# Two-layer FoX and MLA trunk on one core: piecewise first loads, division by head, another bank, another order of end projections, dummy transposes

## The chip, the cores and the metric

The kernel runs on one NeuronCore of a Trainium2 chip, in one launch. The metric is the device time of an execution in microseconds (us); lower is better. All matrix products are made of float32 operands that are each split into two fp32r parts.

## What is computed

A trunk of two layers over x of shape (1, 256, 1024). Each layer is four post-normed steps, with `ALPHA` = sqrt(2):

```python
for i in range(DEPTH):                       # DEPTH = 2, FoX in layer 0, MLA in layer 1
    if i == N_A:
        k_nope, k_rope, v_shared = shared_kv(x, kv_w_down, kv_norm, kv_w_up, cos, sin)
    x = post_norm(x, 0.5 * swiglu(x, ffn1_w_in[i], ffn1_w_out[i]), ...)      # d_ff = 2816
    x = post_norm(x, fox_mixer(...) if i < N_A else mla_mixer(...), ...)     # 16 heads each
    x = post_norm(x, 0.5 * swiglu(x, ffn2_w_in[i], ffn2_w_out[i]), ...)
    gate = sigmoid(x @ ple_w_gate[i] + ple_b_gate[i])
    x = post_norm(x, gate * (p[i] @ ple_w_proj[i]), ...)
```

`swiglu` is `(silu(x Wg) * (x Wu)) Wo`. `fox_mixer` is causal softmax attention with a decay from cumulated log-sigmoids added to the logits; `mla_mixer` takes its keys and values from a shared compressed latent.

## The kernel before, in words

**Numbers.** A float32 operand v is kept as `hi` (v rounded to fp32r, a copy on ScalarE) and `lo` (v minus hi, a subtraction on VectorE). A product is three matmuls, hi·hi, hi·lo and lo·hi, summed in PSUM (`mm3`, L412; all matmuls are recorded at L420, in `mm`). So each weight is loaded, copied on ACT (L140) and subtracted on DVE (L141) before PE can use both parts.

**The weight stream.** `Stream` loads the weights in the order in which a dry run (`Recorder`) saw them used. A group of 1 MB goes from HBM into one of three raw buffers (tile `raw`) by DMAs on SyncE's queue; for FFN input weights (`win`) that is one DMA for the gate columns and one for the up columns. Only the first two groups are loaded in finer pieces: two row blocks (k) per DMA, four DMAs of 256 KB each. A group holds two units; a unit is two row blocks of 128 rows by 512 columns. `split` (L123) turns a unit into the parts in one of up to 14 slots (tiles `hl`, `ota`, `otb`, `qk`, `fs`), whole: one ACT instruction of 128x1024 and one DVE instruction. `use` splits what is needed at once, `pump` splits ahead when its estimates of the engines' time say that there is room; so the order of the instructions on ACT and DVE is set by that planner while the program is written out, and each engine then runs its queue in that order.

**Stages.** Tokens are two tiles t of 128. `XT(t)` transposes x of a tile on PE (eight 128x128 transposes into two `tr` banks, L424) and splits the result into `xT` (L429 on ACT, L430 on DVE). In `ffn` (L509) the first two chunks of 256 hidden columns are made by `H(c, t)` with the tokens as the stationary side (128x512 matmuls, eight row blocks times three per tile), the other nine by `HT` with the weights as the stationary side (128x256 matmuls, 96 a chunk), in the groups 2 to 4, 5 to 7 and 8 to 10; after each group come output projections `W` (128x512 matmuls). `HT` of the chunks 5 and 8 begins with `EDGE[layer, ffn]` dummy transposes of the identity into its first bank. At the program's start `setup` asks for all of x tile 0, then weight group 0, then x tile 1, then group 1, and the first `ffn` (`cold`) does H(0, 0) with `XT(1)` in its middle, then H(0, 1).

**FoX** (L719). `V(n, t)` makes values in a bank of ring `h` (two banks), and its parts on ACT and DVE free that bank. `gen_k` and `gen_q` make a head pair's keys and queries in the same ring `h`. For head pairs j = 0 to 7: `QK(j)` (scores in two `y` banks), `softmax(j)` (L855), `T(j-1)` (transposes of the probabilities, L897 for the first four), `AV(j-1)`. `softmax` takes row maxima of both heads on DVE, four exponentials with sums on ACT (L877: two segments of head 0, then two of head 1), one reciprocal of the four sums on DVE (L882), and four multiplications on GpSimd (POOL, L886).

**MLA** (L1050). For 16 heads, `softmax`, `T(h)`, `AV(h)` and `O(h, ts)`, the head's share of the output projection for the tiles ts, into y. The parts of the last two heads' AV results lie in tile `fs`. After the loop the rest is written out by hand (see the difference below): projections, T(15), AV(15), the layer norm of tile 0 (`ln`), `XT(0)`, the remaining projections of tile 1.

Of the kernel before, what the change touches and what calls it, by code (L numbers as in the profile page):

```python
# [10 lines left out]
F32 = mybir.dt.float32  # L11
# [18 lines left out]
STAG = 3  # L30
LATE = 6
HAT = 12
VAT = 12
SW_COLD = 0
SW_H00 = 0
SW_H10 = 1
SW_H01 = 2
# [9 lines left out]
    (((0, 0),), ((1, 0),), ((0, 1),)),  # L47
)
GROUPS = ((2, 3, 4), (5, 6, 7), (8, 9, 10))
EDGE = {(0, "ffn1"): 4, (0, "ffn2"): 1, (1, "ffn1"): 2, (1, "ffn2"): 1}  # L50
VT = {0: (2, (0,)), 5: (2, (1,)), 8: (3, (0,)), 10: (3, (1,))}


# [13 lines left out]
class Recorder:  # L67
# [7 lines left out]
    def pump(self, *a, **k):  # L75
        pass

    lend = reclaim = check = load = busy = pair = pump


class Stream:


    def __init__(self, nc, raw_pool, pool, loads, seq):
        self.nc, self.raw_pool, self.pool, self.loads = nc, raw_pool, pool, loads
        seen = []
        self.groups = []
        for key in seq:
            g = group_of(key)
            if g not in seen:  # L90
# [12 lines left out]
        self.raw, self.hl = {}, {}  # L103
        self.slots = [f"hl{i}" for i in range(NSLOT)]
        self.slot_of = {}
        self.kept = set()
        self.loaded = self.ready = 0
        self.done = 0
        self.pending = None
        self.pe_t = self.act_t = self.dve_t = self.dma_t = 0.0  # L110
        self.arrives = {}

    def load(self, n=NRAW):
        while self.loaded < len(self.groups) and self.loaded < self.done + n:
            g = self.groups[self.loaded]
            r = self.raw_pool.tile([128, 2048], F32, name="raw")
            self.loads(self.nc.sync, g, r, self.loaded < 2)
# [5 lines left out]
    def split(self):  # L123
# [16 lines left out]
        nc.scalar.activation(hi, src, AF.Copy)  # L140
        nc.vector.tensor_tensor(lo, src, hi.bitcast(F32), op=ALU.subtract)  # L141
# [45 lines left out]

    def pump(self):

        if self.ready == len(self.order) or not self.slots:  # L190
# [33 lines left out]
def unit_of(key, raw):  # L224

    k, u = key[0], key[-1] % 2
    if k in ("win", "fv"):
        return raw.rearrange("p (k c) -> p k c", c=512)[:, 2 * u : 2 * u + 2, :], 128, 1024
    if k in ("wout", "fo", "pg", "pp", "mo", "qr"):
        return raw[:, 1024 * u : 1024 * u + 1024], 128, 1024  # L230
    if k in ("fk", "fq"):
        return raw.rearrange("p (k c) -> p k c", c=256)[:, :, 128 * u : 128 * u + 128], 128, 1024
    if k == "ff":
        return raw[:, 0:1024], 128, 1024
    if k == "pb":
        return raw[0:1, 0:1024], 1, 1024
# [12 lines left out]

def make_loads(a):  # L250
    def rows(ap, k0, n):
        return ap[k0 * 128 : (k0 + n) * 128, :].rearrange("(k p) c -> p k c", p=128)

    def loads(q, g, raw, fine):
        k, i = g[0], g[-1]
        if k == "win":
            w = a[g[2]][0][g[1]]
            c = g[3]
            r = raw.rearrange("p (k c) -> p k c", c=512)
            n = 2 if fine else 4  # L260
            for k0 in range(0, 4, n):
                for s in range(2):
                    c0 = DFF * s + 256 * c
                    q.dma_start(
                        r[:, k0 : k0 + n, 256 * s : 256 * s + 256], rows(w[:, c0 : c0 + 256], 4 * i + k0, n)
                    )
# [69 lines left out]
class Trunk:  # L336
# [33 lines left out]
    def setup(self):  # L370
# [6 lines left out]
        self.ones = one([1, 128], F32R, "ones")  # L377
        self.xT = one([128, 2, 2, 8, 128], F32R, "xT")
        self.rope = one([128, 2, 2, 64], F32, "rope")
        self.load_x(0)  # L380
        self.S.load(1)
        self.load_x(1)
        nc.gpsimd.memset(self.mask, 0.0)
        self.spin(2)
        warm = self.tl([128, 1], F32, "ss", 2)
        nc.gpsimd.memset(self.mhalf, -0.5)
# [17 lines left out]
    def load_x(self, t):  # L404
        for h in range(2):
            self.dma(
                self.x[t][:, 512 * h : 512 * h + 512],
                None if self.rec else self.a["x"][0, 128 * t : 128 * t + 128, 512 * h : 512 * h + 512],
            )


    def mm3(self, out, lhsT, rhs, start, stop):  # L412
# [17 lines left out]
        self.nc.vector.tensor_tensor(lo, src, hi.bitcast(F32), op=ALU.subtract)  # L430
        self.S.pair(cols(src))

    def transposed(self, t, src):

        for h in range(2):
# [10 lines left out]
    def XT(self, t):  # L446
        self.transposed(t, self.x[t])

    def moving(self, ps, t, name, width, at=None, what=None, sweeps=0):

# [58 lines left out]
    def ffn(self, li, which, lni, kv=False, at=None, cold=False):  # L509
# [7 lines left out]
        def H(c, t, at=None, what=None, sweeps=0):  # L517
            ps = self.bank("h")
            self.moving(ps, t, ("win", li, which, c), 512, at, what, sweeps)
            if c not in g:  # L520
# [59 lines left out]
        if kv:  # L580
            self.kv_down(0)
        if cold:
            H(0, 0, 18, lambda: self.XT(1), SW_COLD)
            H(0, 1, sweeps=SW_H01)
            H(1, 0)
        else:
            H(0, 0, sweeps=SW_H00)
# [131 lines left out]
    def fox(self, li):  # L719
# [2 lines left out]
        S.reclaim("ota", "otb")  # L722

        def V(n, t, at=None, what=None):
            ps = self.bank("h")
            self.moving(ps, t, ("fv", n), 512, at, what, {(0, 0): SW_V00, (1, 0): SW_V10, (0, 1): SW_V01}.get((n, t), 0))
            o = self.tl([128, 2, 512], F32R, "g4", 5)
            self.parts(o[:, 0, :], o[:, 1, :], ps)
# [126 lines left out]
        def softmax(j):  # L855
# [26 lines left out]
            nc.vector.reciprocal(su, su)  # L882
            for s in range(2):
                for q, (c0, c1) in enumerate(seg):
                    i = 2 * s + q
                    nc.gpsimd.tensor_scalar(  # L886
                        P[s][:, c0:c1], P[s][:, c0:c1], su[:, i : i + 1], 1.0, op0=ALU.mult, op1=ALU.mult
                    )
            st[j] = P

        def T(j):
# [158 lines left out]
    def mla(self, li):  # L1050
# [206 lines left out]
                AV(h - 1)  # L1257
        self.load_gb(li, 1)
        O(LATE + 2, (1,))
        O(14, (0,))  # L1260
        T(15)
        AV(15)
        O(LATE + 3, (1,))
        O(15, (0,))
        self.ln(0, y[0], ALPHA, LN_EPS)
        for h in range(LATE + 4, 16):
# [5 lines left out]

    def run(self):
        S = self.S
        self.XT(0)
        self.spin(2)
# [74 lines left out]
```

## Time and profile before

| | us |
|---|---|
| Three runs | 1117.63, 1117.82, 1119.79 (median 1117.82) |
| The profiled execution | 1116.59 |
| its span, first to last instruction | 1114.8 |
| PE busy in the span | 1087.3 (98%) |
| DVE, ACT, POOL busy | 712.2, 541.6, 81.8 |
| mean granted TensorE clock | 0.993 |

A timeline row reads: start, length in us, engine, line, operation, out<-in, shape and count; in brackets the idle time of the engine ahead of it and what ended that. Rows that follow each other on one engine at one line are merged. PE's matmuls overlap in the records, so the pace of a stretch is the distance between two starts over the number of matmuls. A row of windows gives for each engine the busy time (and count), then the granted TensorE clock, the DMA share and the GB/s.

### The profile page before, as it was taken

How to read it: one execution, taken by the hardware profiler on the slowest of the kernel's cores; microseconds unless marked ns; L12 is line 12 of the kernel's file. 1: busy time of each engine (PE TensorE's matmuls, PEld its weight loads, DVE VectorE, ACT ScalarE, POOL GpSimd, SP SyncE). 2: the span in 40 equal slices, each digit the busy share in tenths (PEclk: the TensorE clock that was granted, in tenths of full speed). 3: DMA queues.
4: the chain of work that ended last, by engine and by line, in shares of the span. 5: the costliest groups of instructions: out<-in, count | busy, mean ns of one | idle time of the engine just before them, and what ended most of it. 6: DMA issues, size and time to landing. Idle time of an engine off the chain costs nothing. (4 is left out here: it accounts for less than half of the span.)

```text
span 1114.8 us, 17666 instructions
## 1 busy us (share of the span) xinstructions
PE 1087.3 (98%) x7182; PEld 982.3 (88%) x7182; DVE 712.2 (64%) x994; ACT 541.6 (49%) x786; POOL 81.8 (7%) x130
## 2 busy tenths in 40 slices
PE   8999999989999999999999999998999899999997
PEld 6999998889879989897899899987899689898986
DVE  5765545777787555457976454397766786454576
ACT  5554433566646435443565343345655455344421
POOL 0000000322200000000320000011111000000000
PEclk9999999989999999999999999999999999999999
DMA  9796652554338666454486655344443478555402
GB/s 299 240 308 212 216 188 68 171 168 152 114 113 301 200 209 199 159 175 157 155 287 229 204 186 166 88 111 145 156 123 114 158 257 278 185 190 189 164 26 76
DMA packets 150548, 199.00 MB, mean 179 GB/s; under 512 B 11714, under 2 KB 128450, under 8 KB 150468
## 3 DMA queue, kind: packets, MB, share of 16 engines
q1 hardware_dynamic: 150468, 197.88, 53.8%
q8 instruction: 56, 0.92, 0.3%
q14 instruction: 24, 0.20, 0.1%
HBM read 196.81 MB, written 1.05 MB: 177 GB/s over the span
## 5 line engine op out<-in xcount | busy, mean ns | idle before, releaser
L141 DVE TENSOR_TENSOR hl<-raw,hl 128x1024 fp32r<-128x1024 f32 (+3 forms) x295 | 349.3, 1202 | 184.8 <-ACT hl L140 183.7
L140 ACT ACTIVATE hl<-raw 128x1024 fp32r<-128x1024 f32 (+3 forms) x295 | 298.5, 1032 | 208.0 <-PE y L420 85.3
L420 PE MATMUL h<-xT,hl 128*128 128x256 f32 x2016 | 243.3, 281 | 2.4 <-DVE g L430 1.8
L420 PEld LDWEIGHTS h<-xT,hl 128*128 128x128 f32 x2016 | 237.4, 190 | 4.7 <-DVE g L430 2.0
L420 PE MATMUL y<-hl,g 128*128 128x512 f32 x816 | 189.6, 390 | 0.0
L420 PEld LDWEIGHTS y<-hl,g 128*128 128x128 f32 x816 | 152.2, 188 | 31.0
L420 PE MATMUL h<-hl,xT 128*128 128x512 f32 (+1 forms) x432 | 102.1, 387 | 3.3 <-DVE hl L141 1.9
L420 PE MATMUL tr<-xT,hl 128*128 128x256 f32 x864 | 102.5, 278 | 0.0
L420 PEld LDWEIGHTS tr<-xT,hl 128*128 128x128 f32 x864 | 100.5, 188 | 0.1
L420 PEld LDWEIGHTS h<-hl,xT 128*128 128x128 f32 x432 | 79.3, 188 | 21.2 <-DVE hl L141 3.0
L492 POOL TENSOR_TENSOR rs<-ve,mhalf 128x1 f32<-128x1 f32 x16 | 15.2, 950 | 829.4 <-DVE ve L491 829.4
L420 PE MATMUL y<-hl,xT 128*128 128x512 f32 (+2 forms) x276 | 52.6, 346 | 0.0
L420 PEld LDWEIGHTS y<-hl,xT 128*128 128x128 f32 x276 | 44.0, 188 | 6.4 <-issue 0.7
L429 ACT ACTIVATE xT<-tr 128x512 fp32r<-128x512 f32 x36 | 20.0, 596 | 57.0 <-PE tr L424 57.0
L430 DVE TENSOR_TENSOR g<-P,g 128x512 fp32r<-128x512 f32 x36 | 24.9, 693 | 34.5 <-ACT g L429 34.5
L429 ACT ACTIVATE g<-P 128x512 fp32r<-128x512 f32 x36 | 22.8, 632 | 40.1 <-DVE P L559 29.1
L420 PE MATMUL y<-hl,ota 128*128 128x512 f32 x144 | 36.1, 394 | 0.0
L141 DVE TENSOR_TENSOR otb<-raw,otb 128x1024 fp32r<-128x1024 f32 (+1 forms) x20 | 24.1, 1203 | 18.8 <-ACT otb L140 18.8
L141 DVE TENSOR_TENSOR qk<-raw,qk 128x1024 fp32r<-128x1024 f32 x21 | 25.9, 1233 | 14.3 <-ACT qk L140 14.3
L420 PE MATMUL tr<-xT,qk 128*128 128x256 f32 x264 | 31.9, 277 | 0.0
L420 PEld LDWEIGHTS tr<-xT,qk 128*128 128x128 f32 x264 | 30.9, 188 | 0.0
L430 DVE TENSOR_TENSOR xT<-tr,xT 128x512 fp32r<-128x512 f32 x36 | 23.1, 683 | 11.7 <-ACT xT L429 11.7
(222 smaller groups left out, 1349.2 us busy)
## 6 DMA issues: line engine op xcount, KB each, us to landing
raw<-in_ffn_w_in_dram SPq DMA_DIRECT2D x172, 512.0 KB, 4.9
raw<-in_ffn_w_out_dram SPq DMA_DIRECT2D x44, 1024.0 KB, 5.1
raw<-in_fox_w_in_dram SPq DMA_DIRECT2D x12, 1024.0 KB, 5.2
raw<-in_ple_w_gate_dram SPq DMA_DIRECT2D x8, 1024.0 KB, 5.0
raw<-in_mla_w_o_dram SPq DMA_DIRECT2D x8, 1024.0 KB, 5.5
gb<-in_ln_g_dram SPq DMA_DIRECT2D x8, 512.0 KB, 5.1
gb<-in_ln_b_dram SPq DMA_DIRECT2D x8, 512.0 KB, 7.7
raw<-in_fox_w_o_dram SPq DMA_DIRECT2D x4, 1024.0 KB, 4.8
```

The source lines that it names most:

```text
L140: nc.scalar.activation(hi, src, AF.Copy)
L141: nc.vector.tensor_tensor(lo, src, hi.bitcast(F32), op=ALU.subtract)
L420: self.nc.tensor.matmul(out, lhsT, rhs, start=start, stop=stop)
L429: self.nc.scalar.activation(hi, src, AF.Copy)
L430: self.nc.vector.tensor_tensor(lo, src, hi.bitcast(F32), op=ALU.subtract)
L492: nc.gpsimd.tensor_tensor(rs, ve, self.mhalf, op=ALU.pow)
```

## The change

Five edits. (1) The first two weight groups come in pieces of one row block (128 KB a DMA, eight DMAs a group instead of four), the halves of x are put between them, and the first four units are split in two halves (`FINE`); the first chunk for both tiles is written out in `first`, which takes row blocks as they come and puts the four half-`XT`s between them, with the planner on `hold`. (2) In FoX, `softmax` takes the reciprocal and the multiplications head by head. (3) `V(n, 1)` uses a bank of ring `y`. (4) In MLA's end T(15), O(9, tile 1) and AV(15) come ahead of O(14, tile 0). (5) `EDGE` of layer 1's first FFN goes from 2 to 4.

```diff
-EDGE = {(0, "ffn1"): 4, (0, "ffn2"): 1, (1, "ffn1"): 2, (1, "ffn2"): 1}
+EDGE = {(0, "ffn1"): 4, (0, "ffn2"): 1, (1, "ffn1"): 4, (1, "ffn2"): 1}
...
+        def part(c):
+            nc.scalar.activation(hi[:, c], src[:, c], AF.Copy)
+            nc.vector.tensor_tensor(lo[:, c], src[:, c], hi[:, c].bitcast(F32), op=ALU.subtract)
+
+        if self.ready < FINE:
+            part(slice(0, 1))
+            between()
+            part(slice(1, 2))
+        else:
+            part(slice(None))
...
-            n = 2 if fine else 4
+            n = 1 if fine else 4
             for k0 in range(0, 4, n):
+                if fine and (i, k0) in between:
+                    between[i, k0]()
...
-        self.load_x(0)
-        self.S.load(1)
-        self.load_x(1)
+        self.load_x(0, 0)
+        self.S.between = {
+            (0, 2): lambda: self.load_x(1, 0),
+            (1, 0): lambda: self.load_x(0, 1),
+            (1, 1): lambda: self.load_x(1, 1),
+        }
+        self.S.load(2)
...
+        def first():
+
+            ps = [self.bank("h") for _ in range(2)]
+
+            def part(t, *ks):
+                for k in ks:
+                    w = self.use(("win", li, which, 0, k // 2))
+                    for i, j in SWEEPS[0][0]:
+                        self.mm(
...
+            S.hold = True
+            self.XT(0, (0,))
+            self.spin(2)
+            S.split()
+            part(0, 0, 1)
+            S.split(lambda: self.XT(1, (0,)))
+            part(0, 2)
+            part(1, 0, 1)
+            S.split(lambda: self.XT(0, (1,)))
+            part(1, 2)
+            part(0, 3)
+            part(1, 3)
+            self.XT(1, (1,))
+            S.split()
+            part(0, 4, 5, 6, 7)
+            act(0, 0, ps[0])
+            part(1, 4, 5)
+            S.split()
+            S.split()
+            S.hold = False
+            part(1, 6, 7)
+            act(0, 1, ps[1])
...
         if cold:
-            H(0, 0, 18, lambda: self.XT(1), SW_COLD)
-            H(0, 1, sweeps=SW_H01)
+            first()
             H(1, 0)
...
-            ps = self.bank("h")
+            ps = self.bank("h" if t == 0 else "y")
...
-            nc.vector.reciprocal(su, su)
-            for s in range(2):
+
+            def divide(s):
+                nc.vector.reciprocal(su[:, 2 * s : 2 * s + 2], su[:, 2 * s : 2 * s + 2])
...
         O(LATE + 2, (1,))
+        T(15)
+        O(LATE + 3, (1,))
+        AV(15)
         O(14, (0,))
-        T(15)
-        AV(15)
-        O(LATE + 3, (1,))
         O(15, (0,))
```

What stands in the engines' queues, first PE's at the start of the program, before the change. Here x_66 and x_67 are the two tiles of x, and the four `hl` of the first rows are the four units of the first chunk.

```order
L420 MATMUL h<-hl_131,xT 128x512 x6
L420 MATMUL h<-hl_134,xT 128x512 x6
L420 MATMUL h<-hl_149,xT 128x512 x6
L424 MATMUL tr<-ident,x_67 128x128 x8
L420 MATMUL h<-hl_158,xT 128x512 x6
```

The same place of the changed kernel; its four units are hl_130, hl_144, hl_168 and hl_196.

```order
L436 MATMUL h<-hl_130,xT 128x512 x6
L440 MATMUL tr<-ident,x_67 128x128 x4
L436 MATMUL h<-hl_144,xT 128x512 x3
L436 MATMUL h<-hl_130,xT 128x512 x6
L440 MATMUL tr<-ident,x_66 128x128 x4
L436 MATMUL h<-hl_144,xT 128x512 x9
L440 MATMUL tr<-ident,x_67 128x128 x4
L436 MATMUL h<-hl_168,xT 128x512 x6
L436 MATMUL h<-hl_196,xT 128x512 x6
L436 MATMUL h<-hl_168,xT 128x512 x6
L436 MATMUL h<-hl_196,xT 128x512 x6
```

Before, all 24 matmuls of tile 0 stood ahead of those of tile 1; now 24 matmuls of both tiles on the first two units, with the second half of x between them, stand ahead of those on the third and fourth.

DVE at the first softmax of FoX, before; `tt` are the biases of the exponentials and `su` their sums.

```order
L872 TENSOR_TENSOR tt<-nm,cq 128x2
L873 TENSOR_TENSOR tt<-tt,cq 128x2
L882 RECIPROCAL su<-su 128x4
L141 TENSOR_TENSOR hl_2204<-raw,hl_2204 128x1024
L141 TENSOR_TENSOR fs<-raw,fs 128x1024
L430 TENSOR_TENSOR qk<-h,qk 128x256
```

And of the changed kernel:

```order
L927 TENSOR_TENSOR tt<-nm,cq 128x2
L928 TENSOR_TENSOR tt<-tt,cq 128x2
L939 RECIPROCAL su<-su 128x2 x2
L145 TENSOR_TENSOR hl_2221<-raw,hl_2221 128x1024
L145 TENSOR_TENSOR fs<-raw,fs 128x1024
L446 TENSOR_TENSOR qk<-h,qk 128x256
```

One reciprocal became two, the first of which waits for the first head's sums alone; what stands behind them, and POOL's four multiplications, kept their order.

PE at the end of MLA, before; `h<-PT` is AV(15), `tr<-ident,P` is T(15), the rows that end in `fs` are O(14) and O(15), those in `ota` O(8) and O(9).

```order
L420 MATMUL y<-hl_7790,ota 128x512 x6
L420 MATMUL y<-hl_8331,fs 128x512 x6
L424 MATMUL tr<-ident,P 128x128 x3
L420 MATMUL h<-PT,g_7964 128x256 x3
L420 MATMUL h<-PT,g_8108 128x128 x3
L420 MATMUL y<-hl_7815,ota 128x512 x6
L420 MATMUL y<-hl_8375,fs 128x512 x6
```

And of the changed kernel:

```order
L436 MATMUL y<-hl_7818,ota 128x512 x6
L440 MATMUL tr<-ident,P 128x128 x3
L436 MATMUL y<-hl_7843,ota 128x512 x6
L436 MATMUL h<-PT,g_7992 128x256 x3
L436 MATMUL h<-PT,g_8136 128x128 x3
L436 MATMUL y<-hl_8359,fs 128x512 x6
L436 MATMUL y<-hl_8403,fs 128x512 x6
```

O(14, tile 0) moved from ahead of T(15) to behind AV(15), and O(9, tile 1) from behind AV(15) to between T(15) and AV(15).

More of the change, by code (lines that the diff above doesn't have):

```diff
@@ L32 @@
 HAT = 12
+FINE = 4
 VAT = 12
-SW_COLD = 0
 SW_H00 = 0
@@ L76, in pump @@
         pass
-    lend = reclaim = check = load = busy = pair = pump
+    lend = reclaim = check = load = busy = pair = split = pump
+    between, hold = {}, False
 class Stream:
@@ L111, in __init__ @@
         self.arrives = {}
+        self.between = {}
+        self.hold = False
     def load(self, n=NRAW):
@@ L116, in load @@
             r = self.raw_pool.tile([128, 2048], F32, name="raw")
-            self.loads(self.nc.sync, g, r, self.loaded < 2)
+            self.loads(self.nc.sync, g, r, self.loaded < 2, self.between)
             self.raw[g] = r
@@ L121, in load, with split @@
             self.loaded += 1
-    def split(self):
+    def split(self, between=lambda: None):
         nc = self.nc
@@ L139, in split @@
         self.act_t, self.dve_t = max(self.act_t, t), max(self.dve_t, t)
-        nc.scalar.activation(hi, src, AF.Copy)
-        nc.vector.tensor_tensor(lo, src, hi.bitcast(F32), op=ALU.subtract)
+        def part(c):
[7 more added lines that the diff above has]
+            part(slice(None))
         self.pair(n)
@@ L188, in pump @@
     def pump(self):
-        if self.ready == len(self.order) or not self.slots:
+        if self.ready == len(self.order) or not self.slots or self.hold:
             return
@@ L232, in unit_of @@
         return raw.rearrange("p (k c) -> p k c", c=256)[:, :, 128 * u : 128 * u + 128], 128, 1024
+    if k == "pb":
+        return raw[0:1, 0:1024], 1, 1024
     if k == "ff":
         return raw[:, 0:1024], 128, 1024
-    if k == "pb":
-        return raw[0:1, 0:1024], 1, 1024
     if k == "kd":
@@ L252, in rows, with loads @@
         return ap[k0 * 128 : (k0 + n) * 128, :].rearrange("(k p) c -> p k c", p=128)
-    def loads(q, g, raw, fine):
+    def loads(q, g, raw, fine, between):
         k, i = g[0], g[-1]
@@ L402, in spin, with load_x @@
             self.nc.tensor.matmul(hot[:, 0:384], self.mask[:, 0:128], self.mask, start=True, stop=True)
[L404 to L409, printed above, removed]
+    def load_x(self, t, h):
+        self.dma(
+            self.x[t][:, 512 * h : 512 * h + 512],
+            None if self.rec else self.a["x"][0, 128 * t : 128 * t + 128, 512 * h : 512 * h + 512],
+        )
     def mm3(self, out, lhsT, rhs, start, stop):
@@ L431, in parts, with transposed @@
         self.S.pair(cols(src))
-    def transposed(self, t, src):
-        for h in range(2):
+    def transposed(self, t, src, halves=(0, 1)):
+        for h in halves:
             tr = self.bank("tr")
@@ L444, in transposed, with XT @@
             )
-    def XT(self, t):
-        self.transposed(t, self.x[t])
+    def XT(self, t, halves=(0, 1)):
+        self.transposed(t, self.x[t], halves)
     def moving(self, ps, t, name, width, at=None, what=None, sweeps=0):
@@ L519, in H, with act @@
             self.moving(ps, t, ("win", li, which, c), 512, at, what, sweeps)
+            act(c, t, ps)
+        def first():
[5 more added lines that the diff above has]
+                        self.mm(
+                            ps[t], self.xT[:, t, i, k, :], w[:, j, 512 * (k % 2) : 512 * (k % 2) + 512],
+                            k == 0 and (i, j) == (0, 0), k == 7 and (i, j) == SWEEPS[0][0][-1],
+                        )
+                    self.S.pump()
+            S.hold = True
[20 more added lines that the diff above has]
+            act(0, 1, ps[1])
+        def act(c, t, ps):
             if c not in g:
@@ L888, in softmax @@
                     )
+            for s in range(2):
+                divide(s)
             st[j] = P
@@ L1274, in run @@
         S = self.S
-        self.XT(0)
-        self.spin(2)
         keep = lambda *t: (lambda: S.reclaim(*t))
```

## The prediction

> **What bounds the kernel now.** I read the page first: its span, PE's line, then PE's waits, the granted clock by windows, and the timeline at the places that the diff touches.
>
> ```profile
> span 1114.8 us, 17666 instructions
> ...
> PE 1087.3 (98%) x7182; PEld 982.3 (88%) x7182; DVE 712.2 (64%) x994; ACT 541.6 (49%) x786; POOL 81.8 (7%) x130
> ```
>
> PE is busy all but 27.5 us of the span (1114.8 - 1087.3), so only two things can give time: the idle of PE, and the pace at which it runs while busy. The waits of PE name the largest one, and windows of the page's clock record show a price that idle brings with it.
>
> ```profile
> PE tr L897 <- POOL P L886: 3.2, 5, 2.0
> ```
>
> ```profile
> 4.00:14.00 10.00, 6.73 (x27) 4.04 (x26) 4.96 (x5) 5.29 (x6) 0.67 (x3) 1.00 1.05 347
> ...
> 226.00:230.00 4.00, 4.00 (x24) 4.00 (x23) 3.94 (x6) 1.80 (x4) 0.00 (x0) 0.57 0.73 240
> ...
> 243.00:247.00 4.00, 4.00 (x27) 3.78 (x26) 3.40 (x15) 1.41 (x7) 0.00 (x0) 0.57 0.60 244
> ```
>
> In FoX the granted clock is 0.57 on average in two windows of 4 us, each just behind an idle stretch of PE of about 2 us (below). That costs 4 x 0.43 = 1.7 us apiece, on top of the idle. In the start, where PE idles in pieces of about 1 us, the clock stays at 1.00. The Trainium skill ("TensorE: Matmul & The Clock Gate", Part 1) says that the clock halves after an idle window of about 3.4 us; here gaps of 2 us sufficed, so the trace decides. By the page's window the two gaps would have cost no clock, and removing them would gain 1.7 us each less than I count below.
>
> A measurement of this kernel can tell about 0.2% (2.2 us) from no change. The sum is made against the profiled execution, 1116.59 us, of which 1114.8 is its span; it lies 1.23 us below the median of the three runs, 1117.82, so at the end I add 1.23.
>
> **The start.**
>
> ```profile
> 0.72 0.87 SPq L358 DMA_DIRECT2D x<-in_x_dram  x2
> ...
> 3.65 0.94 SPq L358 DMA_DIRECT2D x<-in_x_dram  x2
> ...
> 6.52 1.06 ACT L140 ACTIVATE hl<-raw 128x1024 fp32r<-128x1024 f32 x1 [0.67 <-DMA raw<-in_ffn_w_in_dram]
> ...
> 12.96 1.06 ACT L140 ACTIVATE hl<-raw 128x1024 fp32r<-128x1024 f32 x1 [0.45 <-DMA raw<-in_ffn_w_in_dram]
> ...
> 14.05 1.23 DVE L141 TENSOR_TENSOR hl<-raw,hl 128x1024 fp32r<-128x1024 f32 x1 [0.28 <-ACT hl L140]
> ...
> 15.89 18.10 PE L420 MATMUL h<-hl,xT 128*128 128x512 f32 x78
> ...
> 33.83 0.60 PE L424 MATMUL tr<-ident,P 128*128 128x128 f32 x4
> ```
>
> PE runs without a break only from 15.89; 78 of the 96 matmuls of the first two chunks are left then, and it reaches T(0) at 33.83. The first unit landed at 6.5 and the fourth at 12.96. SyncE issued six DMAs between 0.72 and 3.65, 0.49 each. The new order has 20 DMAs (4 of x, 16 of weights) where 12 were, so the last is issued at about 0.72 + 19 x 0.49 = 10.0; with 2.8 from issue to use (0.72 to about 3.5 for the first half of x) the last row block is there at 12.8, no earlier than now, but the first at about 4.5, and only half of x stands ahead of it. Queued behind the extra issues on SyncE is weight group 2, 4 us later issued than the first row, which PE needs at about 19.5.
>
> Now PE. The first copy of a weight half (1.06 / 2 = 0.53) can end at 5.4, behind the copy of the first half of x. From there 48 matmuls at 18.10 / 78 = 0.232 are 11.1 us, and twelve transposes at 0.60 / 4 = 0.15 are 1.8: never waiting, PE would end H(0, 0) and H(0, 1) at 18.3. The last row block forbids that: its copy stands on ACT behind the copies of the last half of x and of row block 6 and ends at about 15.1, its subtraction on DVE (halves of 1.23) at 16.0; behind it are 15 matmuls, 3.5 us: 19.5. Then 48 more matmuls bring T(0) to 30.6 instead of 33.83: **3.2 us off**. What is late next is DVE: the four units of the second chunk (1.23 each, from 18.1) are ready at 23.2, just ahead of PE. Bounds: 4.2 if the 18.3 holds; 1.1 if the row blocks land 3 us later (rival below).
>
> **FoX.**
>
> ```profile
> 220.15 2.91 PE L420 MATMUL h<-xT,hl 128*128 128x256 f32 x24
> ...
> 224.84 7.35 PE L420 MATMUL h<-xT,hl 128*128 128x256 f32 x48 [1.78 <-DVE g L430]
> ...
> 227.16 0.42 DVE L430 TENSOR_TENSOR qk<-h,qk 128x256 fp32r<-128x256 f32 x1
> ```
>
> The other bank: gen_q(0) waits until 224.84 since its `h` bank still holds V(1, 1), whose `lo` part stands late in DVE's queue. With V(1, 1) in a `y` bank gen_q(0) starts at 222.9 and ends at 225.6. But gen_k(1) takes the bank of gen_k(0), which is freed by the DVE row at 227.16, to 227.58; DVE's queue is the same as before there. So the same 2 us of idle come one step later, and most likely the same halving of the clock behind them: 48 matmuls at 24 per 2.7 us from 222.9 would have ended at 228.4; both ways the end is at about 232. **I count 0**; bounds 0 and 1.7 (no halving this time). A loss is excluded, since no queue moves and `y` has two free banks.
>
> ```profile
> 236.96 0.37 ACT L877 ACTIVATE P<-y,tt 128x128 f32<-128x128 f32 x1
> ...
> 237.91 0.18 DVE L882 RECIPROCAL su<-su 128x4 f32<-128x4 f32 x1 [1.95 <-ACT P L877]
> 238.25 3.65 POOL L886 TENSOR_SCALAR P<-P,su 128x128 f32<-128x128 f32 x4 [15.14 <-DVE su L882]
> ...
> 238.97 0.50 PE L897 MATMUL tr<-ident,P 128*128 128x128 f32 x2
> ...
> 241.22 0.41 DVE L430 TENSOR_TENSOR qk<-h,qk 128x256 fp32r<-128x256 f32 x1
> ...
> 241.50 0.78 PE L897 MATMUL tr<-ident,P 128*128 128x128 f32 x2 [2.03 <-POOL P L886]
> ```
>
> ```profile
> 772.01 0.83 POOL L1175 TENSOR_SCALAR P<-P,su 128x128 f32<-128x128 f32 x2 [8.36 <-DVE su L1173]
> ```
>
> The division: head 0's sums are ready when head 1's exponentials begin (236.96), 0.95 ahead of the reciprocal (237.91), and DVE is idle then. POOL starts at about 237.4 instead of 238.25. Two multiplications beside no subtraction of DVE take 0.83 (772.01); the four here took 3.65, since DVE's subtractions ran from 238.85 on. Started earlier, all four fit into 1.7 to 1.9 us and end at 239.3, when PE has done head 0's two transposes (238.97 + 0.50). The wait of 2.03 falls to 0.2 at most. What is late next is QK(1): its last products need the DVE row at 241.22, done at 241.63, and PE is there at about 240.8. So **1.7 of 2.0** remain; bounds 1.0 and 2.0. Since PE's two gaps are then 0.2 and 0.8 instead of one of 2.0, the halving of 243 to 247 should go: **1.7**, bounds 0 and 1.7. The other four waits of the L897 row (3.2 - 2.0 = 1.2) are of the same kind and shorter than the 0.95: **1.0**, bounds 0.5 and 1.2. The price, eight more reciprocals of 0.18, lies on DVE where it waited for ACT anyway; uncovered it would be 1.4.
>
> **Dummy transposes.**
>
> ```profile
> 94.75 0.60 PE L424 MATMUL tr<-ident 128*128 128x128 f32 x4
> 95.10 11.15 PE L420 MATMUL tr<-xT,hl 128*128 128x256 f32 x96
> ...
> 127.85 16.50 PE L420 MATMUL y<-hl,g 128*128 128x512 f32 x72
> ...
> 632.49 0.38 PE L424 MATMUL tr<-ident 128*128 128x128 f32 x2
> 632.62 11.55 PE L420 MATMUL tr<-xT,hl 128*128 128x256 f32 x96
> ...
> 666.63 16.53 PE L420 MATMUL y<-hl,g 128*128 128x512 f32 x72
> ```
>
> Here PE never waits; the pace differs. Behind four transposes the 288 matmuls of chunks 5 to 7 take 127.85 - 95.10 = 32.75 us (113.7 ns each), behind two 666.63 - 632.62 = 34.01 (118.1). The transposes themselves take 0.35 (94.75 to 95.10) and 0.13. If four bring the fast pace in layer 1 too, each of the two groups of that FFN behind such transposes (chunks 5 to 7 and 8 to 10) gains 1.26 - 0.22 = 1.04: **2.1**. No row says why; bounds 2.1 and a loss of 0.4 (transposes paid, pace unchanged).
>
> **MLA's end.**
>
> ```profile
> 871.08 1.59 PE L420 MATMUL y<-hl,ota 128*128 128x512 f32 x6
> ...
> 872.66 0.82 POOL L1175 TENSOR_SCALAR P<-P,su 128x128 f32<-128x128 f32 x2 [6.69 <-DVE su L1173]
> ...
> 873.57 0.73 PE L420 MATMUL y<-hl,fs 128*128 128x512 f32 x2 [0.90 <-ACT fs L429]
> ...
> 874.81 2.34 DVE L141 TENSOR_TENSOR hl<-raw,hl 128x1024 fp32r<-128x1024 f32 x2
> ...
> 876.00 0.49 PE L424 MATMUL tr<-ident,P 128*128 128x128 f32 x3
> ...
> 877.11 0.56 DVE L430 TENSOR_TENSOR PT<-tr,PT 128x384 fp32r<-128x384 f32 x1
> ...
> 877.72 0.79 PE L420 MATMUL h<-PT,g 128*128 128x256 f32 x5 [0.20 <-DVE PT L430]
> ...
> 879.79 1.53 PE L420 MATMUL y<-hl,fs 128*128 128x512 f32 x6
> 881.15 5.60 PE L420 MATMUL y<-hl,otb 128*128 128x512 f32 x24
> ...
> 888.83 0.63 PE L424 MATMUL tr<-ident,x 128*128 128x128 f32 x4 [0.28 <-DVE x L497]
> ```
>
> O(14) waits for its input and holds back T(15), so AV(15) waits in turn. New: T(15) follows O(8) as soon as POOL is done (873.5); on DVE one subtraction (half of 2.34, to 876.0) stands ahead of the `lo` part of PT (0.56): 876.55, where it was 877.67. O(9) fills PE meanwhile. AV(15) ends at 877.15, then O(14) and O(15) at 1.36 each (879.79 to 881.15): 879.9 instead of 881.15, 1.25 off. The layer norm of tile 0 starts earlier by that and more, as one subtraction less stands ahead of it, so the wait of 0.28 at 888.83 goes too, and the idle of the copies behind it shrinks: **1.8**, bounds 1.0 and 2.5.
>
> **Sum.** 3.2 + 0 + 1.7 + 1.7 + 1.0 + 2.1 + 1.8 = 11.5; 1116.59 - 11.5 = 1105.1, and 1.23 for the median: **1106.3**. All bounds at their worst give 1.1 + 0 + 1.0 + 0 + 0.5 - 0.4 + 1.0 = 3.2 (1114.6), all at their best 15.4 (1102.4).
>
> **Rivals.**
> *The clock is halved in other places.* If the 0.2 and 0.8 us gaps at T(0) and QK(1) still suffice, 1.7 less: 1108.0. For it: they lie within 2.5 us of each other. Against: 1.00 in the start's windows with 3.3 us of idle in 10.
> *The start is bound by its small DMAs.* If the pieces land 3 us later, the last at 15.8, the second chunk's units follow 3 us later and T(0) comes at 32.7: 1.1 instead of 3.2, 1108.4. For it: the DMA share is 1.05 already (row 4 to 14). Against: the two groups and x are 3 MB as before, and at 347 GB/s from 4.0 on that is 8.6 us, so the last would land at 12.6. The Trainium skill ("DMA: Bandwidth & Descriptors", Rules for kernel authors) asks for 1 MiB and more per DMA, and these are 128 KB; the DMAs of the trace overlap, which that rule does not count.
> *The dummy transposes leave the pace as it is*: +2.5, 1108.8. For it: the pace has no shown cause. Against: two groups of two behind four transposes in the same code are fast.
> *Slower:* the shifts throw the FFN matmuls into the slow pace. Each chunk group of three costs 1.26 more; of twelve such groups about eight are fast. With edit 5 void as well (9.0 gained), it decides from the eighth group on; with all eight, and the twelve groups of `W` at the 232 ns of the start's row instead of 229 (16.50 / 72; 72 x 3 ns x 12 = 2.6), it is 1117.8 - 9.0 + 10.1 + 2.6 = 1121.5. For it: the pace hangs on something as small as two transposes. Against: nothing moves in those queues.
>
> **Chances.** Forecast 0.54; clock 0.13; DMAs 0.10; pace unchanged 0.17; pace lost 0.06, of which half ends within 0.2%. One in a hundred for two of the small rivals together bringing it to no change: faster 0.93, same 0.04, slower 0.03. The range goes from 1101.5, 0.9 below the sum of the best bounds, to 1112.0, where two of the small rivals meet with a division at its lower bounds.
>
> **What would show it.** Right: T(0) near 30.6; in FoX no half clock behind T(0), a wait of gen_k(1) for the DVE part of `qk`; four transposes followed by 113.7 ns a matmul in layer 1's first FFN; O(15) of MLA directly behind O(14). Wrong: PE waiting for weights beyond 20 us; waits at L897's successor of 1 us and more; 118 ns behind four transposes; a clock below 1.00 in the first 20 us.

## The result, and the profile after

The changed kernel takes 1109.01 us (median of 5 runs, 1106.37 to 1111.96) where the kernel before, run beside it, takes 1119.26 (1117.63 to 1119.79): a ratio of 0.9911 (95% interval 0.9889 to 0.9933), 0.9% less time. Two repeats on other chips gave 0.9899 (0.9879 to 0.9919) and 0.9902 (0.9887 to 0.9917). The forecast was 1106.3 from 1117.82, a ratio of 0.9897. The profiled execution took 1107.35 where that of before took 1116.59; its page:

```profile
span 1105.6 us, 17707 instructions
...
PE 1082.7 (98%) x7186; PEld 977.1 (88%) x7186; DVE 712.9 (64%) x1006; ACT 542.2 (49%) x790; POOL 75.1 (7%) x130
```

The idle of PE went from 27.5 to 22.9 us (1105.6 - 1082.7), so 4.6 of the 9.2 us is idle and the other half is pace, the speed at which PE runs while it is busy. The table cuts both traces at the last transposes of x of each step; all times are distances between starts on PE.

| stretch | before | after | difference | predicted |
|---|---|---|---|---|
| start to T(0) of the first FFN | 33.83 | 31.39 | -2.44 | -3.2 |
| to the transposes of x in FoX | 168.95 | 170.07 | +1.12 | 0 |
| to those of layer 0's second FFN | 129.16 | 125.73 | -3.43 | -4.4 |
| to those of layer 1's first FFN | 220.80 | 219.27 | -1.53 | 0 |
| to those of MLA | 189.85 | 187.78 | -2.07 | -2.1 |
| to those of layer 1's second FFN | 156.94 | 154.95 | -1.99 | -1.8 |
| to the last of all | 190.79 | 191.89 | +1.10 | 0 |
| to the end of the span | 24.5 | 24.5 | 0.0 | 0 |
| sum | 1114.8 | 1105.6 | -9.2 | -11.5 |

The two rows of layer 1 that had a forecast came out within 0.2 of it. The start and FoX gave 0.8 and 1.0 less than forecast. Three rows that nothing was forecast for moved by more than 1 us each; the experiments below are mostly on these.

The waits of PE in the changed kernel (us in total, times, longest): the row of T waiting for POOL's division in FoX is gone, and the two new waits for `qk` stand where the prediction put them. Not forecast: in MLA, T waits for POOL 1.6 us in three places, where it waited 0.5 in one. One of the two new ones is at T(15) (below); the other, 0.79 at 771.33, is missing in just the four profiles that have a half clock near there.

```profile
PE h L436 <- DVE qk L446: 2.2, 2, 1.9
PE tr L440 <- POOL P L1234: 1.6, 3, 0.8
...
PE y L436 <- DVE qk L446: 0.9, 1, 0.9
```

The windows that the prediction quoted, of the changed kernel (busy time and count by engine, then granted clock, DMA share, GB/s):

```profile
4.00:14.00 10.00, 9.67 (x46) 6.62 (x44) 5.96 (x9) 5.38 (x9) 0.68 (x3) 1.00 0.93 296
226.00:230.00 4.00, 3.68 (x34) 3.51 (x36) 4.00 (x6) 1.30 (x2) 0.00 (x0) 1.00 0.72 217
243.00:247.00 4.00, 4.00 (x36) 3.83 (x35) 2.18 (x9) 3.70 (x11) 1.66 (x4) 1.00 0.02 4
```

In the start PE is busy 9.67 of 10 us instead of 6.73, although the smaller loads moved 296 GB/s there instead of 347. Both windows of FoX ran at full clock: the second as forecast, the first not as forecast.

The start, from the timeline. The prediction had the last row block's subtraction end at 16.0 with 63 matmuls left behind it.

```profile
5.14 0.62 ACT L144 ACTIVATE hl<-raw 128x512 fp32r<-128x512 f32 x1
...
12.52 0.64 ACT L144 ACTIVATE hl<-raw 128x512 fp32r<-128x512 f32 x1 [0.18 <-DMA raw<-in_ffn_w_in_dram]
...
14.76 1.14 ACT L144 ACTIVATE hl<-raw 128x512 fp32r<-128x512 f32 x2
...
15.50 1.28 DVE L145 TENSOR_TENSOR hl<-raw,hl 128x512 fp32r<-128x512 f32 x2
16.24 14.88 PEld L436 LDWEIGHTS h<-hl,xT 128*128 128x128 f32 x65 [0.62 <-DVE hl L145]
16.24 15.32 PE L436 MATMUL h<-hl,xT 128*128 128x512 f32 x65 [0.30 <-DVE hl L145]
...
31.39 0.60 PE L440 MATMUL tr<-ident,P 128*128 128x128 f32 x4
```

The first copy ends at 5.76, 0.36 later than the prediction had it, the last two copies wait for no DMA, and PE waits until 16.24 for the last time, with 65 matmuls left. What it waits for there is the first of the last two subtractions, that of row block 6 (15.50 to 16.18); that of row block 7 ends at 16.78, ahead of the matmul that needs it. From 16.24 to T(0) PE never waits.

FoX: gen_k(1), the multiplications, T(0), and the end of QK(1).

```profile
226.32 3.00 PE L436 MATMUL h<-xT,hl 128*128 128x256 f32 x24 [1.87 <-DVE qk L446]
...
234.58 1.64 POOL L942 TENSOR_SCALAR P<-P,su 128x128 f32<-128x128 f32 x4 [12.78 <-DVE su L939]
...
236.11 0.60 PE L956 MATMUL tr<-ident,P 128*128 128x128 f32 x4
...
238.82 0.50 PE L436 MATMUL y<-qk 64*128 64x128 f32 x4 [0.86 <-DVE qk L446]
```

The idle of before's gen_q(0) stands at gen_k(1), behind DVE's part of `qk`; the four multiplications took 1.64 (forecast 1.7 to 1.9, before 3.65); T(0) waits for nothing, and what is late next is QK(1), by 0.86 (forecast 0.8).

Layer 1's first FFN, behind four transposes: 288 matmuls in 659.38 - 626.63 = 32.75 us, 34.01 before.

```profile
626.28 0.60 PE L440 MATMUL tr<-ident 128*128 128x128 f32 x4
626.63 11.14 PE L436 MATMUL tr<-xT,hl 128*128 128x256 f32 x96
...
659.38 2.90 PE L436 MATMUL y<-hl,g 128*128 128x512 f32 x12
```

MLA's end:

```profile
864.52 0.90 PE L440 MATMUL tr<-ident,P 128*128 128x128 f32 x3 [0.42 <-POOL P L1234]
...
866.25 1.21 DVE L145 TENSOR_TENSOR hl<-raw,hl 128x1024 fp32r<-128x1024 f32 x1
...
867.39 0.55 DVE L446 TENSOR_TENSOR PT<-tr,PT 128x384 fp32r<-128x384 f32 x1
...
867.99 0.79 PE L436 MATMUL h<-PT,g 128*128 128x256 f32 x5 [1.04 <-DVE PT L446]
868.61 2.95 PE L436 MATMUL y<-hl,fs 128*128 128x512 f32 x12
...
871.40 5.60 PE L436 MATMUL y<-hl,otb 128*128 128x512 f32 x24
...
878.20 1.03 PE L440 MATMUL tr<-ident,x 128*128 128x128 f32 x8
```

Two waits, 0.42 at T(15) for POOL and 1.04 at AV(15) behind one weight subtraction on DVE, took the place of five that added up to 2.7; O(14) and O(15) run as one stretch, and the transposes of x at 878.20 no longer wait for the layer norm (0.28 before).

### The profile page after: what moved, and what is told of

The parts are those of the page before. It is cut to its first block, busy times and chain, and to the rows that moved or that the text cites. A ratio compares the mean times of both kernels' runs of the same rounds, so it can differ in the third digit from the quotient of the medians.

```text
span 1105.6 us, 17707 instructions
## 1 busy us (share of the span) xinstructions
PE 1082.7 (98%) x7186; PEld 977.1 (88%) x7186; DVE 712.9 (64%) x1006; ACT 542.2 (49%) x790; POOL 75.1 (7%) x130
## 5 line engine op out<-in xcount | busy, mean ns | idle before, releaser
L436 PE MATMUL h<-xT,hl 128*128 128x256 f32 x2016 | 239.7, 278 | 2.3 <-DVE qk L446 1.9
L436 PEld LDWEIGHTS h<-xT,hl 128*128 128x128 f32 x2016 | 234.0, 188 | 4.1 <-DVE qk L446 2.1
L436 PE MATMUL h<-hl,xT 128*128 128x512 f32 (+1 forms) x396 | 94.7, 389 | 0.5 <-DVE hl L145 0.3
L436 PEld LDWEIGHTS h<-hl,xT 128*128 128x128 f32 x396 | 72.2, 188 | 16.9 <-DVE hl L145 1.9
L436 PE MATMUL y<-hl,xT 128*128 128x512 f32 (+2 forms) x312 | 61.0, 351 | 0.0
L436 PEld LDWEIGHTS y<-hl,xT 128*128 128x128 f32 x312 | 50.8, 188 | 7.9 <-issue 0.7
L436 PEld LDWEIGHTS y<-hl,ota 128*128 128x128 f32 x144 | 26.0, 188 | 5.9 <-ACT P L932 0.9
```

The costliest lines, as they stand in the source:

```text
L436: self.nc.tensor.matmul(out, lhsT, rhs, start=start, stop=stop)
```

## The experiments

All kernels compute the whole reference. There were three groups, each on a chip of its own and each with its own runs of the kernel before (medians 1118.73, 1116.41 and 1116.79 us), so that totals are compared as ratios. Since the edits lie hundreds of microseconds apart, each can also be read from its own stretch of the trace.

**Repeats.** The kernel before, and the changed kernel twice more, with no edit. First the kernel before:

> The kernel before once more, unchanged. If the pace of a group of matmuls and the half-clock windows are set by the program, the profile repeats: groups of (0, ffn2) 31.18, of (1, ffn1) 34.01 and 34.00 us, all others fast, and half clock for 3.4 us at 226, 243 and 776 us. If they are a matter of chance in each execution, at least one of these eight places differs.

The second copy of the changed kernel, and the third:

> The changed kernel once more, unchanged. If pace and clock are set by the program, the profile repeats: no half clock before the end, the first group of (0, ffn1) at 31.18 and the third of (1, ffn2) at 34.46 us, the others fast, span 1105.6. If by chance, some differ, and spans lie between 1104 and 1111, by 1.2 per group and 1.7 per half-clock window. The ratio to the kernel before should be 0.989 to 0.993 either way.

> The changed kernel a third time, as the measure for the other three on the same chip: 0.989 to 0.992 of the kernel before. FoX with idle of 1.9 at gen_k(1) and 0.85 at QK(1) in every profile; whether a half clock follows is chance, 0 or 3.4 us of it.

The profile doesn't repeat, so something other than the program has a part in it. The kernel before was run once here (1116.24 us). Of the places named for it, the first group of (0, ffn2) was fast this time, the third groups of (0, ffn2) and (1, ffn2), fast in the first profile, were slow, and only two of the three half-clock stretches came back (241 and 774 us). The three profiled executions of the changed kernel took 1107.35, 1107.55 and 1104.74; two, two and none of their twelve FFN groups were in the slow pace, and they differ by about that (2 x 1.25 = 2.5). The same stretch of the third group of (0, ffn2), in windows of PE alone, of the changed kernel's first profile and of its second:

```profile
465.00:485.00 20.00, 20.00 (x178) 1.00 0.46 159
```

```profile
465.00:485.00 20.00, 20.00 (x172) 1.00 0.44 159
```

PE is busy throughout at clock 1.00 in both, and does six matmuls fewer in the second. In the traces, the distance between the starts of neighbouring matmuls is 113.3 ns on average or 117.8 ns; which one is settled within the first dozen matmuls of the group, and it then holds for all of the group's 288. That is what the prediction had averaged and called the pace behind four or two transposes.

**The dummy transposes alone.**

```diff
-EDGE = {(0, "ffn1"): 4, (0, "ffn2"): 1, (1, "ffn1"): 2, (1, "ffn2"): 1}
+EDGE = {(0, "ffn1"): 4, (0, "ffn2"): 1, (1, "ffn1"): 4, (1, "ffn2"): 1}
```

> The kernel before with four dummy transposes instead of two in layer 1's first FFN, nothing else. If the number of transposes sets the pace, both groups run 288 matmuls in 32.75 us instead of 34.01, and the whole is 2.1 us faster (0.19%). If the pace is fallen into by chance, whatever the number, one or both groups stay at 34.0, and the whole is 0.4 slower to 1.0 faster.

Ratio 0.9964 (0.9951 to 0.9978). Both groups are fast, and the stretch of this FFN takes 187.70 us where it took 189.85. The ratio (4.0 us) says more than this stretch, which gives 2.1; where the rest comes from, this profile doesn't show.

**Four transposes at all groups**, on the changed kernel:

```diff
-EDGE = {(0, "ffn1"): 4, (0, "ffn2"): 1, (1, "ffn1"): 4, (1, "ffn2"): 1}
+EDGE = {(0, "ffn1"): 4, (0, "ffn2"): 4, (1, "ffn1"): 4, (1, "ffn2"): 4}
```

> The changed kernel with four dummy transposes instead of one in both second FFNs as well. In the profiles so far groups behind four transposes were always in the fast pace, groups behind two always in the slow one, and the last groups of the second FFNs, behind one, in either. If four transposes bring the fast pace, all eight such groups take 32.75 us (33.2 with the wait of 0.5 in the third group of the second FFNs), and the kernel is 0.4 to 1.2 us faster than the changed kernel, 0.989 to 0.991 of the kernel before. If the pace has nothing to do with the number, one or more of them are slow and it is 0.5 to 1.3 us slower than the changed kernel.

Ratio 0.9946 (0.9933 to 0.9960): no better than the changed kernel, on the ratios of other chips worse. Four are no guarantee (the second group of (0, ffn2), fast behind one in all 13 other profiles, ran at 117.8 behind four), and the planner's splits moved: in layer 1's second FFN two weight subtractions now stand on DVE ahead of the product that frees the second bank of chunk 2, so PE waits there, six matmuls behind T(0).

```profile
905.67 2.36 DVE L145 TENSOR_TENSOR hl<-raw,hl 128x1024 fp32r<-128x1024 f32 x2 [1.87 <-ACT hl L144]
...
908.41 2.39 PE L436 MATMUL h<-xT,hl 128*128 128x256 f32 x18 [1.52 <-DVE P L580]
```

**Four at the third groups of the second FFNs only**, on the changed kernel:

```diff
-HT(c, (lambda: T(1)) if c == 2 else None, EDGE[li, which] if c == group[0] > 2 else 0)
+HT(c, (lambda: T(1)) if c == 2 else None, (4 if c == 8 else EDGE[li, which]) if c == group[0] > 2 else 0)
```

> The changed kernel with four dummy transposes instead of one ahead of the third chunk group of both second FFNs, where one transpose was followed by the fast pace in some profiles and by the slow one in others; the second groups, always fast behind one, keep it. If four bring the fast pace, both third groups run at 113.3 ns and the kernel is 0.6 us faster than the changed one per execution in which one of them was slow, up to 2.0 us where both were (0.0 to 0.18%). If pace is chance whatever the number, no difference within 0.1%; if the dummies shift the planner's splits into a wait as four at all groups did at 908 us, 1 to 2 us slower.

Ratio 0.9921 (0.9907 to 0.9935) where the changed kernel had 0.9902 on the same chip. Both third groups were fast, but the same wait of 1.6 us for the product came at 908 us, as the third theory has it. Over all fourteen profiles of this study, groups by the number of transposes ahead of them:

| transposes ahead | groups in the fast pace |
|---|---|
| 4, first FFNs | 44 of 44 |
| 2, layer 1's first FFN | 0 of 12 |
| 1, second groups of the second FFNs | 26 of 26 |
| 1, third groups of the second FFNs | 11 of 22 |
| 4, second groups of the second FFNs | 1 of 2 |
| 4, third groups of the second FFNs | 6 of 6 |
| none, first groups (chunks 2 to 4) | 53 of 56 |

The table is no clean test of the number. Two transposes stand in one FFN only, and four almost only in first FFNs. In the third groups of the second FFNs PE waits, behind one transpose, for a bank that a copy on ACT still holds (0.19 to 0.20 us, at the seventh matmul), and the pace that stays is the one in which it starts again after that; with four transposes this wait is gone. The same row of the changed kernel's first profile, slow, and of its third, fast:

```profile
1020.89 5.21 PE L436 MATMUL h<-xT,hl 128*128 128x256 f32 x42 [0.20 <-ACT ota L703]
```

```profile
1019.52 5.04 PE L436 MATMUL h<-xT,hl 128*128 128x256 f32 x42 [0.19 <-ACT ota L703]
```

Nor is each group a toss of its own: in 10 of the 11 profiles with one transpose there, the two third groups are both fast or both slow. In the ten slow groups of these pairs, the starts on the two sides of the wait lie 473 or 474 ns apart, in the ten fast ones 475. So a nanosecond or two at the restart goes with the pace; what sets it for a whole execution was not found.

**The start alone**, on the kernel before (the first edit of the change, whole).

> The kernel before with the new start alone. If the start is worth what the prediction says, T(0) of the first FFN begins at 30.6 to 31.4 us instead of 33.83, and the whole is 2.4 to 3.2 us faster, provided that the pace of the chunks 2 to 4 behind it stays at 113.3 ns. If the new start itself throws these chunks into the slow pace, as in the changed kernel's profile (31.18 us for the stretch instead of 30.02), 1.2 us of it are given back and the whole is 1.2 to 2.0 faster; all else, with its three half-clock windows, as in the kernel before.

Ratio 0.9977 (0.9963 to 0.9992). T(0) begins at 31.45, just past the 30.6 to 31.4 that were expected. Over all profiles T(0) begins at 33.23 to 33.91 with the old start (six) and at 31.39 to 32.17 with the new one (eight): 1.96 between the means. Chunks 2 to 4 were fast behind it here and in six of the seven other profiles with the new start, so the new start does not put them in the slow pace.

**The division alone.**

```diff
-            nc.vector.reciprocal(su, su)
-            for s in range(2):
+            def divide(s):
+                nc.vector.reciprocal(su[:, 2 * s : 2 * s + 2], su[:, 2 * s : 2 * s + 2])
...
+            for s in range(2):
+                divide(s)
```

> The kernel before with the division head by head alone. If the wait of T(0) came from the common reciprocal, the idle of 2.0 us at T(0) of FoX falls to 0.2 at most, the wait moves to QK(1) (0.8 to 0.9 us), the four multiplications take about 1.7 us instead of 3.65, and no half clock follows it: 2.0 to 4.4 us faster as a whole (0.18 to 0.39%). If POOL would be as slow beside DVE as before, T(0) still waits 1 us or more and the gain is under 1 us. The wait of gen_q(0), 1.8 us, and with it the chance of a half clock of 1.7 us behind it, stays.

Ratio 0.9969 (0.9960 to 0.9978), in the forecast interval.

```profile
224.23 5.82 PE L420 MATMUL h<-xT,hl 128*128 128x256 f32 x48 [1.77 <-DVE g L430]
...
236.83 0.60 PE L901 MATMUL tr<-ident,P 128*128 128x128 f32 x4
...
239.52 0.49 PE L420 MATMUL y<-qk 64*128 64x128 f32 x4 [0.84 <-DVE qk L430]
```

T(0) waits for nothing, QK(1) for 0.84. The stretch of FoX takes 125.65 us, as in all three profiles of the changed kernel (125.65 to 125.73), with no half clock. The wait of gen_q(0) is untouched and 1.77 long, and here no half clock follows it.

**The other bank alone.**

```diff
-            ps = self.bank("h")
+            ps = self.bank("h" if t == 0 else "y")
```

> The kernel before with V(n, 1) in a bank of ring y alone. If the wait only moves, gen_q(0) starts at once and gen_k(1) waits 1.8 to 1.9 us for the DVE part of qk instead; T(0) keeps its 2.0: no difference beyond the chance of a half clock, -0.15 to +0.15%. If the freed bank were worth something by itself, the idle between V(1, 1) and gates_transpose would fall by 1 us or more.

Ratio 1.0005 (0.9994 to 1.0016): nothing, and the wait moved as said.

```profile
227.65 3.00 PE L420 MATMUL h<-xT,hl 128*128 128x256 f32 x24 [1.87 <-DVE qk L430]
```

**MLA's end alone.**

```diff
-        O(14, (0,))
         T(15)
-        AV(15)
         O(LATE + 3, (1,))
+        AV(15)
+        O(14, (0,))
```

> The kernel before with the new order of MLA's end alone. If the order is what counts, the stretch from T(15) to O(15)'s end is 1.0 to 2.5 us shorter, as the changed kernel's profile has it (1.8 to 1.9), the waits there fall from five to one of about 1.0 at AV(15): 0.09 to 0.22% faster. If the gain came with the earlier start of the loads, which the other edits shift, there is none here (0 to 0.5 us).

Ratio 0.9966 (0.9948 to 0.9984). The stretch of MLA takes 155.45 us instead of 156.94, a gain of 1.5; waits of 0.18 and 0.29 remain behind the layer norm, where the changed kernel has one of 0.20. The ratio says more than this stretch (3.8 us); this profile doesn't show the rest.

**No splits between gen_k(0) and gen_k(1)**, an attempt on FoX's last wait, on the changed kernel:

```diff
+        S.hold = True
         gen_k(0)
         gen_q(0)
...
                 gen_k(j + 1)
+                S.hold = False
```

> The changed kernel with no weight split ahead between gen_k(0) and gen_k(1) of FoX, so that DVE has the lo parts of qk at once. If the wait of 1.9 us at gen_k(1) comes from weight subtractions that stand ahead of the lo part, it falls to under 0.5 and the kernel is 1.0 to 2.0 us faster (0.09 to 0.18%), and no half clock can follow that place. If the four units that are put off are missed later, PE waits for them at QK(0), gen_k(2) or behind, by up to 2.4 us in sum, and nothing is gained.

Ratio 0.9926 (0.9914 to 0.9939), against 0.9902 on the same chip: slower. The wait of gen_k(1) does fall, to 0.60 (under 0.5 was expected), but four subtractions of 1.2 us each come later, ahead of what QK and AV need.

```profile
224.73 3.00 PE L436 MATMUL h<-xT,hl 128*128 128x256 f32 x24 [0.60 <-DVE qk L446]
...
247.80 0.49 PE L436 MATMUL y<-qk 64*128 64x128 f32 x4 [0.79 <-DVE qk L446]
```

FoX takes 128.97 us instead of 125.70. The second of its two rivals was right.

**Both of these attempts together.**

> Both edits of the two other kernels on the changed one. If they are independent, 1.0 to 4.0 us faster than the changed kernel: 0.986 to 0.990 of the kernel before where the changed one has 0.990. If the planner's later splits move with them, one of the two gains goes again, and it equals the better of the two or less.

Ratio 0.9939 (0.9926 to 0.9951): worse than either. All twelve groups were fast and no half clock came before the end, and still its profile takes 1109.43 against 1104.74 of the changed kernel in the same condition. Its product in layer 1's second FFN is late too, by 0.73. No version here beats the changed kernel.

**The half clock, over all profiles.** Where the granted clock is 0.5 ahead of the program's end, it is so for 3.41 us or twice that, and the halved stretches of a trace lie whole multiples of that apart (in the kernel before, the second begins 13.65 us, 4 x 3.413, behind the end of the first). So I cut the traces at these lengths from the edges of a halved stretch and looked at the idle in the piece before. Of the kernel before, the piece at gen_q(0) and the next one; then of the division alone:

```profile
222.82:226.23 3.41, 1.62 (x15) 1.43 (x14) 3.31 (x6) 3.06 (x6) 0.29 (x1) 1.00 0.67 205
226.23:229.64 3.41, 3.41 (x19) 3.41 (x18) 3.35 (x5) 1.21 (x3) 0.00 (x0) 0.50 0.73 258
```

```profile
221.26:224.67 3.41, 1.64 (x14) 1.44 (x13) 3.34 (x5) 2.11 (x5) 1.25 (x1) 1.00 0.77 266
224.67:228.09 3.42, 3.42 (x32) 3.42 (x31) 3.33 (x6) 2.54 (x4) 0.00 (x0) 1.00 0.96 299
```

The same idle, 1.8 of 3.41, was followed by half clock once and not the other time. Between the first 8 us and the last matmul, a piece with 2.03 idle or more was followed by it in 4 of 4 cases, with 1.5 to 1.9 in 4 of 8, with 1.28 to 1.5 in 4 of 14, these all at MLA's place near 772 us, and with less in none (pieces that were halved themselves are left out). A gap of 1.87 us that falls across the edge of two pieces leaves neither with enough: in the changed kernel's second and third profiles 0.9 and 1.0, 0.8 and 1.1. The Trainium skill ("TensorE: Matmul & The Clock Gate", Part 1) says that the window is free-running, which these cuts bear out; it also speaks of an idle window of about 3.4 us, and here half of one was enough.

## Why the prediction was right, and where its sizes were off

- **The start, 3.2.** Right in kind and in order, too large by 0.8 in this profile and by 1.2 over all. The step at fault is the one that named the last wait: the prediction had PE wait for the last row block until 16.0 with 63 matmuls left, but PE waited for the row block ahead of it until 16.24 with 65 left (0.24 and 2 x 0.233 = 0.47). The rival of late DMAs is not what took it: the last two copies, at 14.76, wait for no DMA. On ACT they stand behind the copies of x, as said.
- **The other bank, 0.** Right: 1.0005 with this edit alone. The half clock behind it, "most likely the same", was wrong for the profile: it came in one of the six profiles that have the gap of 1.9 at gen_k(1) (226.8 us, with four transposes at the third groups). Its absence gave 1.5 us of FoX that no term claimed, which was luck: the kernel before takes 127.61 there without it and 129.16 with it.
- **The division, 1.7 + 1.7 + 1.0.** The places came out as forecast, T(0) without its wait and QK(1) late by 0.86. That is 2.03 - 0.86 = 1.2; the prediction worked out the 0.8 at QK(1) and still kept 1.7 of 2.0, which is the step that failed. The half clock at 243 to 247 went, but was not worth 1.7: with the old division FoX takes 127.17 without any half clock, 127.61 with one at T(0), and 129.0 to 129.2 with two. Behind a slow PE the next waits for POOL shrink, so the halved stretch at T(0) cost 0.4 and not 1.7 (from T(0) to the end of AV(0) the kernel with it lost 1.5, and at T(2), where POOL's wait was gone, it won 0.8 back); the one at gen_k(1), behind which no wait got shorter (QK(1) waits 0.85 there), cost 1.6 (127.27 against 125.70). The four later waits of T went as well, but two others came (0.45 and 0.34 at the last head pair), and with no half clock on either side the whole edit is worth 127.17 - 125.65 = 1.5.
- **Dummy transposes, 2.1.** Right in size (2.07; 189.84 to 189.92 in six profiles with two, 187.70 to 187.87 in eight with four). Right for this FFN, not as the rule that it looked like: see the table of groups. That "no row says why" still stands. The cause of the two paces was not found.
- **MLA's end, 1.8.** Right, 1.99 in the profile, 2.2 in the other two of the changed kernel, 1.5 with this edit alone. The half clock near 776 in the kernel before cost nothing there: the stretch takes 156.94 with it and 156.95 without, since T's wait of 0.8 for POOL is gone behind it.
- **Nothing elsewhere.** Wrong by chance, and only a repeat shows it: +1.12, -1.53 and +1.10 are groups of matmuls that fell into the other pace (31.18 instead of 30.02 us for the first group of (0, ffn1), the reverse for that of (0, ffn2), 34.46 instead of 33.22 for the third of (1, ffn2)); 0.4 of the -1.53 is left over. The rival "pace lost" had the mechanism, but not as something that the edits do.

In sum: without the chances the change is worth 2.0 + 1.5 + 2.1 + 2.0 = 7.6 us by its stretches, where the forecast had 11.5. The medians of the three comparisons say 10 to 11. That they came so near the forecast is in part luck: about 3 us of them belong to no term of its sum. Part of these is that the kernel before draws more half clocks: its gap of 2.0 us at T(0) brought one or two in five of the six profiles with the old division, for 0.4 to 2.0 us, and no profile with the new one has any there. MLA's end is such a place too: one of the six profiles with the old order has a half clock there (the start alone, 6.83 us from 873.0), and its stretch takes 159.37 us instead of 156.94 to 157.00; none of the eight with the new order has one. What makes up the remainder was not measured apart. The ratios of the single edits say more than their stretches as well: they add up to 1.2%.

Three slips in the working changed nothing. The units of the second chunk come to 23.0 (18.1 + 4 x 1.23) and not 23.2; nine of the twelve groups of before's profile are fast, not about eight; and where the prediction speaks of 1.7 us less for each of two gaps, its sum counted only one.

## What to carry to other kernels

Read a stretch of matmuls by the distance between their starts, not by busy time: PE was "busy" at clock 1.00 in both paces, 4% apart. Before a difference of 1 us between two profiles is explained, profile the same kernel twice, and count what each profile drew by chance before a median that fits is taken for a sum that fits. And where a planner fills an engine's queue from estimates, a small edit also moves work that it doesn't name: each of the four kernels here that held splits back or added transposes met a new wait of DVE, and none beat the changed kernel.

## What the runs showed of the hardware

- Two steady paces of 128x256 matmuls with a weight load each, 113.3 and 117.8 ns at clock 1.00, settled within the first dozen behind a change of stream or a wait and held for 33 us.
- Behind two transposes of the identity a group was in the slow pace in 12 of 12 cases (all in one FFN), behind four in the fast one in 51 of 52; behind one, second groups were fast in 26 of 26 and third groups in 11 of 22. That the number is the cause is not shown.
- The clock was halved for multiples of 3.41 us behind pieces that were idle by 1.3 to 2.2 us, at places that change from one execution to the next; one of 3.41 us cost from nothing to 1.6, by what PE would have waited for behind it.
- GpSimd's four multiplications took 1.64 us ahead of DVE's subtractions and 3.65 beside them.
